# Raw weight loads over three buffer rings, a final norm whose last square is summed by TensorE, and three preparations held behind the bank sums

## The chip, the cores and the metric

The kernel runs on one core of one Trainium2 chip. The metric is the device time of one execution in microseconds (us): median of three runs. Besides the timed runs there is one profiled execution, from which all rows of the trace come.

## What is computed

One decoder layer on `x` of 1 x 1024 positions x 1024 channels, in float32:

```
h = rmsnorm(x, norm1_w);  proj = h @ w_in
A: short convolution, gated delta rule, gated norm     B: dilated window attention
x = x + concat(A, B) @ w_out
h = rmsnorm(x, norm2_w)
u = causal_dwconv(h @ w_up, ffn_conv_w)                # 2 x 2816 channels
gate, up = u[..., :2816], u[..., 2816:]
x = x + (silu(gate) * up) @ w_down                     # 2816 -> 1024: the down projection
out = rmsnorm(x, final_norm_w)
```

Only the last two lines, the down projection and the final norm, are touched by the change.

## The kernel before

Everything is held transposed: 128 channels on the partitions, positions along the free axis. Every matrix product is made three times over: an operand is split into a high part (a rounded copy made by ScalarE, ACT) and a low part (the rest, a subtraction on VectorE, DVE), and TensorE (PE) multiplies high x high, high x low and low x high (`mm3`). So each operand of the down projection has to be prepared: loaded by a DMA that SyncE (SP) issues, combined, copied by ACT, subtracted by DVE.

**The down projection** (`mlp_down`) is one level of a fast (seven product) matrix scheme. The 22 blocks of 128 channels are paired into HT = 11 steps `j`. There are four stages of 11 steps. In stages 0, 1 and 2 each step feeds two products, one into the four PSUM banks `pa`, one into the four banks `pb` (two tags of two banks each; all banks are called `dw` in the trace); a product of a step is 12 matmuls of 128x512. Stage 3 has one product, into `pa`; its last LAST = 5 steps are done bank by bank in two halves of 256 positions (`last_product`), so that the final norm of the left half can run while the right half is multiplied. At the end of a stage each of the eight banks is added into the residual stream in SBUF (`add_to`, rows `x1h<-x1h,dw`, one per bank), and the first matmul of the next stage into a bank has to wait until that bank has been read: these are the bank sums.

**Preparation.** `prep(stage, j)` is called one step ahead of its products. Stage 0 loads weights (`wd`, 512 KB) and activations (`r`, from the DRAM buffer `upark`), and splits both. Stage 1 loads a weight pair `wd` and half a pair `wa` (256 KB), makes two combinations of weights and one of activations (`t2 = q1 - r0`), splits three tiles, and updates `r`. Stage 2 loads two pairs and combines them. Stage 3 loads half a pair. The split tiles are called `pr` and take turns over 11 tags (`PTAGS`, nine in pool tag Xb, two in Xa); a `pr` buffer is free again when PE has read it for the last time.

**Raw weight buffers.** Three tags of the pool `wp` have two buffers of 4 KB per partition each: `wst`, `whi`, `wlo`. Stage 0 used `wst` and `whi` in turn, stage 1 `wst` for `wd`, `whi` for `wa` and `wlo` for `t2`, stage 2 `wst` and `whi`, stage 3 `wst` and `whi` in turn. In the up projection before it, `wst` and `whi` hold raw weights and `wlo` the tile `u2`. A load into a buffer starts when the last reader of its former content is done.

**The order of instructions.** PE's order is fixed by the program (an issue token on every matmul). The order on DVE, ACT and SP is made by the tile framework's scheduler, which walks a timeline of its own when the program is built and issues what it thinks is ready; each engine then runs its list strictly in order. `after(inst, anchor)` adds an ordering edge for that scheduler: `inst` comes later than `anchor` in the list, with no new semaphore on the same engine. SP's list holds all DMA issues: one that waits for a buffer holds up those behind it.

**The end.** For a half of 256 positions `complete` squares each of the eight row blocks on ACT and adds the squares into `rstdB` on DVE; `final_norm` sums over the partitions by matmuls with a column of ones (`ps<-ones,rstdB`), makes the scale on DVE and GpSimd (POOL, `rs`), spreads it over the partitions by transposes (`ps<-ident,rs`), and eight DVE instructions scale the row blocks (`x1h<-x1h,fw,ps`), each followed by a DMA to the output (`out_xT`, 128 KB each).

Of the kernel before, what the change touches and what calls it, by code (L numbers as in the profile page):

```python
# [7 lines left out]
F32 = mybir.dt.float32  # L8
# [136 lines left out]
def hybrid_layer(tc, I, out):  # L145
# [7 lines left out]
    po_ = Engine(wv, nc.gpsimd, "gpsimd", 0.15, 0.0021)  # L153
    sy = Engine(wv, nc.sync, "sync", 0.05, 0.00142, 2.2)
    es = ExitStack()
    cp = es.enter_context(tc.tile_pool(name="cp", bufs=1))
# [1195 lines left out]

    def raw_tile(name, tag, src, n=2):
        t = tile_(wp, [P, n, 512], F32, name, tag, 2)
        sy.dma_start(t, src)
        return t
# [10 lines left out]
    def split_pair(src):  # L1367
        hi, lo = [], []
        for d in (hi, lo):
            d.append(A("pr", PTAGS[pcount[0] % len(PTAGS)], F32R, (P, 2, 512)))  # L1370
            pcount[0] += 1
        split_block((hi[0], lo[0]), src)
        return [(hi[0][:, i, :], lo[0][:, i, :]) for i in range(2)]

    def split_one(src, tag=None):
        if tag is None:
            tag = PTAGS[pcount[0] % len(PTAGS)]
            pcount[0] += 1
        t = A("pr", tag, F32R, (P, 2, 512))
        b = t[:, 0, :], t[:, 1, :]  # L1380
        split_block(b, src)
        return b

    def prep(stage, j):
        if stage == 0:

            g = raw_tile("wd", ("wst", "whi")[j % 2], wd_rows(j, 0))
            r = R1[j] = acts("r1", R1TAGS[j], j, 0)
# [4 lines left out]
        elif stage == 1:  # L1393

            u = raw_tile("wd", "wst", wd_rows(j, 1))
            a = raw_tile("wa", "whi", wd_rows(j, 0)[:, 0:1], 1)
            r, q = R1[j], R2[j]
            sy.dma_start(q[:, 1, :], upark[HT + j][:, half(1)])
            t2 = tile_(wp, [P, 512], F32, "t2", "wlo", 2)
            ve.tensor_tensor(u[:, 1, :], u[:, 0, :], u[:, 1, :], op=OP.add)  # L1400
            ve.tensor_tensor(u[:, 0, :], u[:, 1, :], a[:, 0, :], op=OP.subtract)
            ve.tensor_tensor(t2, q[:, 1, :], r[:, 0, :], op=OP.subtract)
            w = split_pair(u)
            ops[stage, j] = [(w[0], split_one(t2)), (w[1], split_one(r[:, 0, :]))]
            ve.tensor_tensor(r[:, 1, :], r[:, 1, :], t2, op=OP.subtract)
        elif stage == 2:

            g = raw_tile("wd", "wst", wd_rows(j, 0))
            u = raw_tile("wd", "whi", wd_rows(j, 1))
            ve.tensor_tensor(g, g, u, op=OP.subtract)  # L1410
            ve.tensor_tensor(g[:, 1, :], g[:, 0, :], g[:, 1, :], op=OP.add)
            r = R2[j]
            ve.tensor_tensor(r[:, 0, :], r[:, 1, :], r[:, 0, :], op=OP.subtract)
            ops[stage, j] = list(zip(split_pair(g), split_pair(r)))
        else:

            a = raw_tile("wa", ("wst", "whi")[j % 2], wd_rows(j, 1)[:, 1:2], 1)
            ops[stage, j] = [(split_one(a[:, 0, :]), split_one(R1[j][:, 1, :], R2TAGS[j]))]
# [15 lines left out]
    def add_to(pd, m, hh, sl):  # L1434
        x = x1h[m][:, part(m, hh, sl)]
        ve.tensor_tensor(x, x, pd[:, sl], op=OP.add)

    def complete(m, hh, sl):

        sp_ = part(m, hh, sl)  # L1440
        x = x1h[m][:, sp_]
        sq = tile_(sp, [P, 512], F32, "sq3", "t2", 2)
        ac.activation(sq[:, sl] if m else rstdB[:, sp_], x, AF.Square)
        if m:
            ve.tensor_tensor(rstdB[:, sp_], rstdB[:, sp_], sq[:, sl], op=OP.add)

    def final_norm(hh, sl, tags, between=None):
        n_ = (sl.stop - sl.start) // P
        ss = bank(tags[0])
        for c in range(n_):  # L1450
            o = 512 * hh + sl.start + c * P
            mm(ss[:, c:c + 1], rstdB[:, o:o + P], ones[:, :1], 0.215)
        rs = tile_(sp, [P, 4], F32, "rs3", "rs3", 2)
        ve.tensor_scalar(rs[:, :n_], ss[:, :n_], 1.0 / 1024, EPS, op0=OP.mult, op1=OP.add)
        rsqrt(rs[:, :n_], rs[:, :n_], n_)
        if between is not None:
            between()
        pb = bank(tags[1])
        for c in range(n_):
            tp(pb[:, c * P:(c + 1) * P], rs[:, c:c + 1].to_broadcast([P, P]))  # L1460
        for m in range(8):
            x = x1h[m][:, part(m, hh, sl)]
            ve.scalar_tensor_tensor(x, x, fw[:, m:m + 1], pb[:, :sl.stop - sl.start], op0=OP.mult, op1=OP.mult)
            sy.dma_start(out[m * P:(m + 1) * P, part(m, hh, sl)], x)

# [5 lines left out]
    def mlp_down():  # L1471
# [30 lines left out]
        def last_product(i, sl):  # L1502
            for j in range(HT - LAST, HT):
                down(pa[i], i, ops[3, j][0], sl, False, j == HT - 1)
            add_to(pa[i], 4 + i, 0, sl)
            complete(4 + i, 0, sl)


# [3 lines left out]
        last_product(0, right)  # L1512
        final_norm(0, left, ("hf", "ch"), lambda: last_product(1, right))
        for i in (2, 3):
            last_product(i, right)
        final_norm(0, right, ("hf", "ch"))

# [71 lines left out]
```

## Time and profile before

| | us |
|---|---|
| median of three runs | 1220.66 (1220.21 to 1220.72) |
| the profiled execution | 1219.28 |
| its span, first to last instruction | 1217.5 |
| PE busy in the span | 1200.4 |
| DVE busy | 946.1 |
| ACT busy | 574.6 |
| POOL busy | 52.1 |
| first product of the down projection | at 988.74 |
| last product of the down projection ends | at 1205.35 |

All times in rows are us from the start of the span. A row of a timeline gives start, duration, engine, source line, operation, the tiles written and read (buffer numbers left out), the shape, how many instructions were merged into the row, and in brackets the idle time of the engine just before it and what ended it. Lines L139, L141, L189 and L193 are helpers through which every operation passes, so rows are told apart by their tiles. SPq is the queue of DMA issues. A DVE row of 128x512 lasts 0.68 to 0.69 us, but the next one starts 0.60 us after it; one of 128x1024 lasts 1.22 and the next starts after 1.14: what counts in a queue is the step from start to start.

### The profile page before, as it was taken

How to read it: one execution, taken by the hardware profiler on the slowest of the kernel's cores; microseconds unless marked ns; L12 is line 12 of the kernel's file. 1: busy time of each engine (PE TensorE's matmuls, PEld its weight loads, DVE VectorE, ACT ScalarE, POOL GpSimd, SP SyncE). 2: the span in 40 equal slices, each digit the busy share in tenths (PEclk: the TensorE clock that was granted, in tenths of full speed). 3: DMA queues.
4: the chain of work that ended last, by engine and by line, in shares of the span. 5: the costliest groups of instructions: out<-in, count | busy, mean ns of one | idle time of the engine just before them, and what ended most of it. 6: DMA issues, size and time to landing. Idle time of an engine off the chain costs nothing.

```text
span 1217.5 us, 18285 instructions
## 1 busy us (share of the span) xinstructions
PE 1200.4 (99%) x7064; PEld 986.3 (81%) x7064; DVE 946.1 (78%) x1459; ACT 574.6 (47%) x1124; POOL 52.1 (4%) x46
## 2 busy tenths in 40 slices
PE   9999999999999999999999999999999999999996
PEld 7878887889777778888888888888888888787886
DVE  7675965566477686767989988989889889899875
ACT  7393344356344453655544544445444444344441
POOL 0311010003100000000000000000000000000000
PEclk9999999999999999999999999999999999999998
DMA  7425252335634213444213223132231496555623
GB/s 231 107 79 165 83 145 85 116 127 164 214 102 129 88 36 107 173 139 144 82 57 105 68 88 104 52 104 68 89 104 53 141 376 234 165 177 177 181 87 139
DMA packets 85799, 154.81 MB, mean 127 GB/s; under 512 B 21168, under 2 KB 36304, under 8 KB 85712
## 3 DMA queue, kind: packets, MB, share of 16 engines
q1 hardware_dynamic: 85712, 153.64, 39.4%
q8 instruction: 55, 0.90, 0.3%
q14 instruction: 32, 0.26, 0.1%
HBM read 117.68 MB, written 35.93 MB: 126 GB/s over the span
## 4 chain that ended last, share of the span: by engine, by line
PE 87%; DVE 6%; DMA 3%; issue 2%; ACT 2%; SPq 0%; POOLq 0%; POOL 0%; DVEq 0%; ACTq 0%
PE ps L189 44%; PE pa L189 20%; PE pc L189 10%; PE dw L189 10%; PE ps L193 3%; DMA wd<-in_wd 2%; DVE pr L139 2%; DVE x1h L139 1%; DVE wd L139 1%; DVE kT L139 1%; ACT dec L139 1%; PE warm L189 1%; DVE wlo L139 0%; DMA r<-upark 0%; ACT sq L141 0%
## 5 line engine op out<-in xcount | busy, mean ns | idle before, releaser
L189 PE MATMUL dw<-pr 128*128 128x512 f32 (+1 forms) x984 | 213.0, 377 | 2.2 <-DVE x1h L139 2.2
L189 PEld LDWEIGHTS dw<-pr 128*128 128x128 f32 x984 | 176.1, 188 | 38.0 <-DVE x1h L139 4.4
L189 PE MATMUL ps<-xhi,whi 128*128 128x512 f32 x384 | 158.5, 413 | 0.0
L189 PE MATMUL ps<-xhi,wlo 128*128 128x512 f32 x384 | 150.3, 391 | 0.0
L189 PE MATMUL ps<-xlo,whi 128*128 128x512 f32 x384 | 150.1, 391 | 0.0
L189 PE MATMUL pa<-T,pair 128*128 128x512 f32 x528 | 127.1, 389 | 0.0
L189 PEld LDWEIGHTS pa<-T,pair 128*128 128x128 f32 x528 | 99.0, 188 | 20.5
L189 PEld LDWEIGHTS ps<-xhi,wlo 128*128 128x128 f32 x384 | 72.1, 188 | 15.7 <-DVE wlo L139 0.2
L189 PEld LDWEIGHTS ps<-xhi,whi 128*128 128x128 f32 x384 | 72.3, 188 | 14.9 <-issue 1.4
L189 PEld LDWEIGHTS ps<-xlo,whi 128*128 128x128 f32 x384 | 72.4, 189 | 12.1 <-DVE xlo L139 0.3
L139 ACT ACTIVATE u<-pa 128x512 f32<-128x512 f32 x44 | 26.3, 599 | 109.5 <-PE pa L189 109.5
L139 ACT ACTIVATE whi<-wst 128x1024 fp32r<-128x1024 f32 (+2 forms) x41 | 41.9, 1021 | 73.8 <-PE ps L189 65.9
L139 DVE SCALAR_TENSOR_TENSOR y<-xu,fcw,y 128x1023 f32<-128x1023 f32 (+1 forms) x44 | 56.3, 1281 | 22.1 <-ACT y L139 22.0
L141 ACT ACTIVATE sm<-sm,mx 128x128 f32<-128x128 f32 (+7 forms) x64 | 35.4, 555 | 60.0 <-DVE mx L141 60.0
L189 PE MATMUL pa<-T,S 128*128 128x512 f32 x264 | 63.4, 389 | 0.0
L189 PE MATMUL pa<-B,A 128*128 128x512 f32 x264 | 63.4, 389 | 0.0
L189 PE MATMUL pc<-T,S 128*128 128x512 f32 x264 | 63.4, 389 | 0.0
L189 PE MATMUL pc<-B,pair 128*128 128x512 f32 x264 | 63.4, 389 | 0.0
L139 DVE TENSOR_TENSOR wst<-wst 128x512 f32<-128x512 f32 x88 | 60.5, 687 | 0.9
L189 PE MATMUL ps<-B,pair 128*128 128x512 f32 x252 | 60.5, 389 | 0.0
L139 ACT ACTIVATE pr<-wd 128x1024 fp32r<-128x1024 f32 x33 | 34.9, 1058 | 50.5 <-DVE wd L139 28.0
L139 DVE TENSOR_TENSOR wlo<-wst,whi 128x1024 fp32r<-128x1024 f32 (+2 forms) x41 | 48.2, 1175 | 13.1 <-ACT whi L139 13.1
(245 smaller groups left out, 2360.9 us busy)
## 6 DMA issues: line engine op xcount, KB each, us to landing
wst<-in_wu SPq DMA_DIRECT2D x44, 512.0 KB, 3.7
wd<-in_wd SPq DMA_DIRECT2D x44, 512.0 KB, 4.3
upark<-y SPq DMA_DIRECT2D x22, 512.0 KB, 3.7
wst<-in_wi SPq DMA_DIRECT2D x21, 512.0 KB, 3.7
r<-upark SPq DMA_DIRECT2D x11, 512.0 KB, 7.9
r<-upark SPq DMA_DIRECT2D x22, 256.0 KB, 7.0
wa<-in_wd SPq DMA_DIRECT2D x22, 256.0 KB, 2.7
wst<-in_wv SPq DMA_DIRECT2D x8, 512.0 KB, 3.5
```

The costliest lines, as they stand in the source:

```text
L139: return getattr(eng, op)(*a, **kw)
L141: return getattr(eng, op)(*a, **kw)
L189: tc.stamp_issue_order_token(nc.tensor.matmul(dst, lhs, rhs, start=start, stop=stop, **kw).ins, TOKEN)
L193: tc.stamp_issue_order_token(nc.tensor.transpose(dst, src, ident if idt is None else idt).ins, TOKEN)
```

## The change

Four things change; the products and their order on PE stay as they are.

1. All raw weight tiles of the down projection take turns over the three tags (`wd_tile`), six buffers in all. In stage 1 the tile `wa` is a whole pair, of which one half takes the load and the other takes `t2`, so that a step of stage 1 holds two buffers where it held three.
2. Three preparations get an ordering edge to the last bank sum of the stage before (`behind`): the making of `t2` of step (1, 4) and the last low part of step (1, 1) come after sum number 7, the last of stage 0; the last low part of step (2, 1) comes after sum number 15, the last of stage 1.
3. The final norm is cut into `mean_of`, `turned` and `scale_out`. The scalings of the left half are placed by hand: row blocks 0 to 3, then the bank sum of product 2 of the right half, row blocks 4 to 6, the bank sum of product 3, row block 7. The square of the very last row block is not added into `rstdB`: TensorE sums it by two further matmuls with ones into the same bank.
4. The last eight output DMAs are issued from SP and ACT in turn (`queues=(sy, sa)`).

```diff
--- before.py
+++ after.py
@@ -152,6 +152,7 @@
     ua = Engine(wv, nc.scalar, "scalar", 0.12, 0.00085, first=tc.high_priority)
     po_ = Engine(wv, nc.gpsimd, "gpsimd", 0.15, 0.0021)
     sy = Engine(wv, nc.sync, "sync", 0.05, 0.00142, 2.2)
+    sa = Engine(wv, nc.scalar, "actq", 0.05, 0.00142, 2.2)
     es = ExitStack()
     cp = es.enter_context(tc.tile_pool(name="cp", bufs=1))
     wp = es.enter_context(tc.tile_pool(name="wp", bufs=1))
@@ -1350,8 +1351,14 @@
     pcount = [0]
     LAST = 5
 
-    def raw_tile(name, tag, src, n=2):
-        t = tile_(wp, [P, n, 512], F32, name, tag, 2)
+    wcount = [0]
+
+    def wd_tile(name="wd"):
+        wcount[0] += 1
+        return tile_(wp, [P, 2, 512], F32, name, ("wst", "whi", "wlo")[wcount[0] % 3], 2)
+
+    def raw_tile(src):
+        t = wd_tile()
         sy.dma_start(t, src)
         return t
 
@@ -1369,7 +1376,7 @@
         for d in (hi, lo):
             d.append(A("pr", PTAGS[pcount[0] % len(PTAGS)], F32R, (P, 2, 512)))
             pcount[0] += 1
-        split_block((hi[0], lo[0]), src)
+        lows.append(split_block((hi[0], lo[0]), src)[1])
         return [(hi[0][:, i, :], lo[0][:, i, :]) for i in range(2)]
 
     def split_one(src, tag=None):
@@ -1378,13 +1385,18 @@
             pcount[0] += 1
         t = A("pr", tag, F32R, (P, 2, 512))
         b = t[:, 0, :], t[:, 1, :]
-        split_block(b, src)
+        lows.append(split_block(b, src)[1])
         return b
+
+    lows, added = [], []
+
+    def behind(inst, n):
+        after(inst, added[n], "the banks of the stage are added first")
 
     def prep(stage, j):
         if stage == 0:
 
-            g = raw_tile("wd", ("wst", "whi")[j % 2], wd_rows(j, 0))
+            g = raw_tile(wd_rows(j, 0))
             r = R1[j] = acts("r1", R1TAGS[j], j, 0)
             ops[stage, j] = list(zip(split_pair(g), split_pair(r)))
             q = R2[j] = A("r2", R2TAGS[j], shape=(P, 2, 512))
@@ -1392,29 +1404,37 @@
             ve.tensor_tensor(r[:, 0, :], q[:, 0, :], r[:, 0, :], op=OP.subtract)
         elif stage == 1:
 
-            u = raw_tile("wd", "wst", wd_rows(j, 1))
-            a = raw_tile("wa", "whi", wd_rows(j, 0)[:, 0:1], 1)
+            u = raw_tile(wd_rows(j, 1))
+            both = wd_tile("wa")
+            sy.dma_start(both[:, 0, :], wd_rows(j, 0)[:, 0, :])
             r, q = R1[j], R2[j]
             sy.dma_start(q[:, 1, :], upark[HT + j][:, half(1)])
-            t2 = tile_(wp, [P, 512], F32, "t2", "wlo", 2)
+            t2 = both[:, 1, :]
             ve.tensor_tensor(u[:, 1, :], u[:, 0, :], u[:, 1, :], op=OP.add)
-            ve.tensor_tensor(u[:, 0, :], u[:, 1, :], a[:, 0, :], op=OP.subtract)
-            ve.tensor_tensor(t2, q[:, 1, :], r[:, 0, :], op=OP.subtract)
+            ve.tensor_tensor(u[:, 0, :], u[:, 1, :], both[:, 0, :], op=OP.subtract)
+            inst = ve.tensor_tensor(t2, q[:, 1, :], r[:, 0, :], op=OP.subtract)
             w = split_pair(u)
             ops[stage, j] = [(w[0], split_one(t2)), (w[1], split_one(r[:, 0, :]))]
+            if j == 4:
+                behind(inst, 7)
+            if j == 1:
+                behind(lows[-1], 7)
             ve.tensor_tensor(r[:, 1, :], r[:, 1, :], t2, op=OP.subtract)
         elif stage == 2:
 
-            g = raw_tile("wd", "wst", wd_rows(j, 0))
-            u = raw_tile("wd", "whi", wd_rows(j, 1))
+            g = raw_tile(wd_rows(j, 0))
+            u = raw_tile(wd_rows(j, 1))
             ve.tensor_tensor(g, g, u, op=OP.subtract)
             ve.tensor_tensor(g[:, 1, :], g[:, 0, :], g[:, 1, :], op=OP.add)
             r = R2[j]
             ve.tensor_tensor(r[:, 0, :], r[:, 1, :], r[:, 0, :], op=OP.subtract)
             ops[stage, j] = list(zip(split_pair(g), split_pair(r)))
+            if j == 1:
+                behind(lows[-1], 15)
         else:
 
-            a = raw_tile("wa", ("wst", "whi")[j % 2], wd_rows(j, 1)[:, 1:2], 1)
+            a = wd_tile("wa")
+            sy.dma_start(a[:, 0, :], wd_rows(j, 1)[:, 1, :])
             ops[stage, j] = [(split_one(a[:, 0, :]), split_one(R1[j][:, 1, :], R2TAGS[j]))]
 
     def load_x1(mg, hh):
@@ -1433,35 +1453,52 @@
 
     def add_to(pd, m, hh, sl):
         x = x1h[m][:, part(m, hh, sl)]
-        ve.tensor_tensor(x, x, pd[:, sl], op=OP.add)
-
-    def complete(m, hh, sl):
+        added.append(ve.tensor_tensor(x, x, pd[:, sl], op=OP.add))
+        return added[-1]
+
+    def complete(m, hh, sl, apart=False):
 
         sp_ = part(m, hh, sl)
         x = x1h[m][:, sp_]
         sq = tile_(sp, [P, 512], F32, "sq3", "t2", 2)
         ac.activation(sq[:, sl] if m else rstdB[:, sp_], x, AF.Square)
+        if apart:
+            return sq
         if m:
             ve.tensor_tensor(rstdB[:, sp_], rstdB[:, sp_], sq[:, sl], op=OP.add)
 
+    def mean_of(hh, sl, tag, more=None):
+        n_ = (sl.stop - sl.start) // P
+        ss = bank(tag)
+        for src, o in ((rstdB, 512 * hh + sl.start), (more, sl.start)):
+            if src is not None:
+                for c in range(n_):
+                    mm(ss[:, c:c + 1], src[:, o + c * P:o + c * P + P], ones[:, :1], 0.215,
+                       src is rstdB and (c == 0 or more is None), src is more or more is None, skip_group_check=True)
+        rs = tile_(sp, [P, 4], F32, "rs3", "rs3", 2)
+        uv.tensor_scalar(rs[:, :n_], ss[:, :n_], 1.0 / 1024, EPS, op0=OP.mult, op1=OP.add)
+        rsqrt(rs[:, :n_], rs[:, :n_], n_)
+        return rs
+
+    def turned(rs, sl, tag):
+        pb = bank(tag)
+        for c in range((sl.stop - sl.start) // P):
+            tp(pb[:, c * P:(c + 1) * P], rs[:, c:c + 1].to_broadcast([P, P]))
+        return pb
+
+    def scale_out(hh, sl, pb, ms=range(8), queues=(sy,), anchor=None):
+        for m in ms:
+            x = x1h[m][:, part(m, hh, sl)]
+            inst = ve.scalar_tensor_tensor(x, x, fw[:, m:m + 1], pb[:, :sl.stop - sl.start], op0=OP.mult, op1=OP.mult)
+            if anchor is not None:
+                after(inst, anchor, "the sums of the last banks go first")
+            queues[m % len(queues)].dma_start(out[m * P:(m + 1) * P, part(m, hh, sl)], x)
+
     def final_norm(hh, sl, tags, between=None):
-        n_ = (sl.stop - sl.start) // P
-        ss = bank(tags[0])
-        for c in range(n_):
-            o = 512 * hh + sl.start + c * P
-            mm(ss[:, c:c + 1], rstdB[:, o:o + P], ones[:, :1], 0.215)
-        rs = tile_(sp, [P, 4], F32, "rs3", "rs3", 2)
-        ve.tensor_scalar(rs[:, :n_], ss[:, :n_], 1.0 / 1024, EPS, op0=OP.mult, op1=OP.add)
-        rsqrt(rs[:, :n_], rs[:, :n_], n_)
+        rs = mean_of(hh, sl, tags[0])
         if between is not None:
             between()
-        pb = bank(tags[1])
-        for c in range(n_):
-            tp(pb[:, c * P:(c + 1) * P], rs[:, c:c + 1].to_broadcast([P, P]))
-        for m in range(8):
-            x = x1h[m][:, part(m, hh, sl)]
-            ve.scalar_tensor_tensor(x, x, fw[:, m:m + 1], pb[:, :sl.stop - sl.start], op0=OP.mult, op1=OP.mult)
-            sy.dma_start(out[m * P:(m + 1) * P, part(m, hh, sl)], x)
+        scale_out(hh, sl, turned(rs, sl, tags[1]))
 
     STEPS = [(s_, j) for s_ in range(4) for j in range(HT)]
     XLOADS = {6: (0, 0), 12: (1, 0), 14: (0, 1), 16: (1, 1)}
@@ -1502,18 +1539,22 @@
         def last_product(i, sl):
             for j in range(HT - LAST, HT):
                 down(pa[i], i, ops[3, j][0], sl, False, j == HT - 1)
-            add_to(pa[i], 4 + i, 0, sl)
-            complete(4 + i, 0, sl)
-
+            total = add_to(pa[i], 4 + i, 0, sl)
+            return total, complete(4 + i, 0, sl, sl.start > 0 and i == 3)
 
         left, right = slice(0, 256), slice(256, 512)
         for i in range(4):
             last_product(i, left)
         last_product(0, right)
-        final_norm(0, left, ("hf", "ch"), lambda: last_product(1, right))
-        for i in (2, 3):
-            last_product(i, right)
-        final_norm(0, right, ("hf", "ch"))
+        rs = mean_of(0, left, "hf")
+        last_product(1, right)
+        pl = turned(rs, left, "ch")
+        scale_out(0, left, pl, range(0, 4))
+        third, _ = last_product(2, right)
+        scale_out(0, left, pl, range(4, 7), anchor=third)
+        fourth, more = last_product(3, right)
+        scale_out(0, left, pl, range(7, 8), anchor=fourth)
+        scale_out(0, right, turned(mean_of(0, right, "hf", more), right, "ch"), queues=(sy, sa))
 
     wv.add(0, norms())
     wv.add(1, gates())
```

## The prediction

> **What bounds the kernel now.** I first read who PE waited for in the stretch from the down projection to the end, then PE's own timeline there. The columns of the first view are total, times and longest wait; the view is cut to this stretch.
>
> ```profile
> span 1217.5 us, 18285 instructions
> PE dw L189 <- DVE x1h L139: 2.2, 5, 0.6
> 988.74 61.41 PE L189 MATMUL dw<-pr 128*128 128x512 f32 x270
> 1050.76 0.96 PE L189 MATMUL dw<-pr 128*128 128x512 f32 x3 [0.61 <-DVE x1h L139]
> 1051.96 3.06 PE L189 MATMUL dw<-pr 128*128 128x512 f32 x12 [0.23 <-DVE x1h L139]
> 1055.55 57.42 PE L189 MATMUL dw<-pr 128*128 128x512 f32 x252 [0.53 <-DVE x1h L139]
> 1113.36 3.06 PE L189 MATMUL dw<-pr 128*128 128x512 f32 x12 [0.39 <-DVE x1h L139]
> 1116.89 68.99 PE L189 MATMUL dw<-pr 128*128 128x512 f32 x303 [0.47 <-DVE x1h L139]
> ```
>
> PE is the bound, and it never waits for an operand: it stops five times, 0.61 + 0.23 + 0.53 = 1.37 us around the end of stage 0 and 0.39 + 0.47 = 0.86 around the end of stage 1, each time for a bank sum, 2.23 in all. After its last product (1201.52 + 3.83 = 1205.35, a row of the tail below) a chain of 12.15 us follows. The change can win there: at two stage ends and in that tail. A product matmul takes 61.41 / 270 = 0.227, so a step of 24 takes 5.45, a product of 12 takes 2.72, and stage 0 (264) ends at 988.74 + 60.0 = 1048.7.
>
> Why the sums are late shows DVE's timeline at the first stage end, and ACT's and SP's ahead of it:
>
> ```profile
> 1037.68 1.06 ACT L139 ACTIVATE pr<-wd 128x1024 fp32r<-128x1024 f32 x1 [4.15 <-PE dw L189]
> 1041.71 0.38 SPq L139 DMA_DIRECT2D wd<-in_wd  x1
> 1045.88 0.69 DVE L139 TENSOR_TENSOR wd<-wd 128x512 f32<-128x512 f32 x1 [2.14 <-DMA wd<-in_wd]
> ...
> 1047.69 1.28 DVE L139 TENSOR_TENSOR x1h<-x1h,dw 128x512 f32<-128x512 f32 x2
> 1048.88 1.22 DVE L139 TENSOR_TENSOR pr<-wd,pr 128x1024 fp32r<-128x1024 f32 x1
> 1050.02 0.68 DVE L139 TENSOR_TENSOR x1h<-x1h,dw 128x512 f32<-128x512 f32 x1
> ...
> 1053.61 0.68 DVE L139 TENSOR_TENSOR t<-r,r 128x512 f32<-128x512 f32 x1
> 1054.21 0.69 DVE L139 TENSOR_TENSOR pr<-r,pr 128x512 fp32r<-128x512 f32 x1
> 1054.82 0.68 DVE L139 TENSOR_TENSOR x1h<-x1h,dw 128x512 f32<-128x512 f32 x1
> DVE wd L139 <- DMA wd<-in_wd: 13.8, 12, 2.7
> ```
>
> The first bank was full at about 1048.7 - 5.45 + 0.68 = 1043.9, but DVE stood still for 2.14 us until a raw weight load landed, and started that sum at 1047.69 (a row that merges sums 1 and 2). The third sum (1050.02) ends at 1050.70, while PE wants its bank 6 matmuls into stage 1, at 1050.1: the stall of 0.61. Two preparations (`t<-r,r`, `pr<-r,pr`) stand ahead of the eighth: the stall of 0.53. Over the down projection up to 1190 DVE waited 13.8 us in 12 pieces for raw weights (last row, DVE's waits).
>
> **Change 1 and 2 at the first stage end.** The change turns two buffers per kind into six shared ones and puts the `t2` of step (1, 4) and the last low part of (1, 1) behind the eighth sum. I walk through DVE's new list there; steps from start to start are 1.28 - 0.68 = 0.60 for 128x512, and 1050.02 - 1048.88 = 1.14 for 128x1024. The low part of (1, 0) needs ACT's copy, which waits for a buffer that PE gives back, as now at 1037.68; so it is done at 1037.68 + 1.06 + 1.22 = 1040.0. It frees the buffer of the load for (1, 3), which lands 1045.88 - 1041.71 = 4.2 us later, at 1044.2. The new list stands still for that too, but then has only a combination and a low part ahead of the first sum: 1045.4. Then follow a combination, sum 2 (1046.6), a low part of 1.14, sum 3 (1048.3), a low part, sum 4 (1049.5), sums 5 to 8 (1050.1 to 1051.9). Done 0.68 later, sum 3 is there 1.1 us before PE wants it, sum 4 (wanted at 1050.8) 0.6, sum 8 (wanted at 1053.5) 0.9. So all three stalls go, with about half a microsecond to spare. Behind the sums the held low part of (1, 1) runs at 1052.5; PE wants it with the second product of that step, at 1048.7 + 5.45 + 2.72 = 1056.9. What waits behind it on DVE belongs to steps (1, 2) and later. The edges cost nothing while that slack of 4 us lasts.
>
> **The second stage end.**
>
> ```profile
> 1109.09 1.88 DVE L139 TENSOR_TENSOR x1h<-x1h,dw 128x512 f32<-128x512 f32 x3
> ...
> 1115.02 1.22 DVE L139 TENSOR_TENSOR pr<-r,pr 128x1024 fp32r<-128x1024 f32 x1
> 1116.15 0.68 DVE L139 TENSOR_TENSOR x1h<-x1h,dw 128x512 f32<-128x512 f32 x1
> ```
>
> Without stalls stage 1 now ends 1.4 us earlier, at 1108.7, so DVE must be earlier by as much. In the list of before stand 55 short and 14 long instructions between the last sum of stage 0 and the first of stage 1: 55 x 0.60 + 14 x 1.14 = 49.0; it took 1055.4 to 1109.1, so 4.7 us of waits. The new list has 54 and 15, 49.5 us, from 1052.5: the first sum comes at 1102.0 plus waits. Sum 3 follows 4.1 us behind sum 1 (a low part, two combinations and two sums stand between), lasts 0.68 and is wanted at 1108.7 + 1.36 = 1110.1: up to 3.3 us of waits do no harm. Loads now have three steps of lead instead of two, 5.45 us more for a transfer of 4.2; the waits that are left are for `pr` buffers, which PE hands back at its own pace. I take 2 us. The low part of (2, 1) that stood ahead of the eighth sum (1115.02) goes behind it, at about 1110, and is wanted at 1114.2. So 0.86 goes too. Together **-2.2**, with bounds of 0 (the stalls stay as large) and -2.23.
>
> **Stage 0.** Here the ring order moves loads on SP's queue: the weights of step 6 are issued before the activations of steps 1, 3 and 5, and those of step 4 wait for `u2` of the last up tile, holding up what stands behind them on SP.
>
> ```profile
> 985.00:1021.00 36.00, 36.00 (x161) 29.78 (x160) 33.49 (x38) 17.87 (x18) 0.00 (x0) 1.00 0.99 358
> 1003.85 1.22 DVE L139 TENSOR_TENSOR pr<-r,pr 128x1024 fp32r<-128x1024 f32 x1
> ```
>
> The DMA engines are 0.99 busy at 358 GB/s (last columns), so 512 KB put ahead cost 1.5 us. The low part of (0, 3) ends at 1005.07, just when PE wants it (988.74 + 3 x 5.45 = 1005.1). But in the new list four short instructions (the `t2` and `r` updates of steps 0 and 1) no longer stand before it, 2.4 us, and ACT copies `xu` before it waits for step 1's activations. A load late by 1.5 us is covered: 0, bounds 0 to +1.5.
>
> **Change 3 and 4, the tail.**
>
> ```profile
> 1201.92 3.22 DVE L139 SCALAR_TENSOR_TENSOR x1h<-x1h,fw,ps 128x256 f32<-128x256 f32 x8
> 1205.05 0.42 DVE L139 TENSOR_TENSOR rstdB<-rstdB,sq 128x256 f32<-128x256 f32 x1
> 1205.39 0.74 DVE L139 TENSOR_TENSOR x1h<-x1h,dw 128x256 f32<-128x256 f32 x2
> 1206.34 0.96 DVE L139 TENSOR_TENSOR rstdB<-rstdB,sq 128x256 f32<-128x256 f32 x2 [0.21 <-ACT sq L139]
> 1199.04 0.61 PE L189 MATMUL ps<-ones,rstdB 128*128 128x1 f32 x4
> 1199.51 2.03 PE L189 MATMUL dw<-pr 128*128 128x256 f32 x15
> 1201.38 0.38 PE L193 MATMUL ps<-ident,rs 128*128 128x128 f32 x2
> 1201.52 3.83 PE L189 MATMUL dw<-pr 128*128 128x256 f32 x30
> 1207.44 0.98 PE L189 MATMUL ps<-ones,rstdB 128*128 128x1 f32 x4 [2.10 <-DVE rstdB L139]
> 1209.53 0.69 PE L193 MATMUL ps<-ident,rs 128*128 128x128 f32 x2 [1.10 <-POOL rs L139]
> 1205.89 0.75 ACT L139 ACTIVATE sq<-x1h 128x256 f32<-128x256 f32 x2 [3.38 <-DVE x1h L139]
> 1207.40:1209.50 2.10, 0.98 (x4) 0.93 (x4) 0.16 (x1) 0.00 (x0) 0.69 (x1) 0.50 0.00 0
> L139 SPq DMA_DIRECT2D out_xT<-x1h x8: 332/390/404, 1210.8 to 1214.1; - x8
> ```
>
> The hand-placed scalings move the last bank sum hardly at all: four scalings of (1205.05 - 1201.92) / 8 = 0.39, an add into `rstdB`, the sum of product 2, three scalings, an add, each add 1205.39 - 1205.05 = 0.34, and then the last sum at 1201.92 + 7 x 0.39 + 3 x 0.34 = 1205.67, where it now starts at 1206.13 - 0.42 = 1205.71. Its square is ready at about 1206.6 (now 1206.64). Now two adds follow it, up to 1207.30, and the ones matmuls start 0.14 later. In the new version they follow the square directly, 1206.73 at the earliest: **-0.7**. The four extra ones matmuls (on `rstdB`) run before that.
>
> The ones matmuls took 0.98 at a granted clock of 0.50 (window row), and 0.61 at full clock (1199.04). Starting 0.7 earlier, behind ones matmuls at about 1205.9, I let them run at full clock: **-0.4**. The transposes (0.69, and 0.38 at full clock) I leave as they are. The Trainium skill, "TensorE: Matmul & The Clock Gate", section "What's actually happening", says that the clock falls only after a free-running window of about 3.4 us without activity. The trace has half clock from 2.1 us after the last product on, so the figure does not fit here. By the rule the transposes would stay fast as well, and the time would be 0.3 lower.
>
> The eight last issues go out every (1214.1 - 1210.8) / 7 = 0.47 us, while DVE scales every 0.39; the last is issued 1214.1, 0.6 later than its scaling allows (1210.8 + 7 x 0.39 = 1213.5). With two queues each has 0.78 per issue: **-0.6**. What an issue costs on ACT no row shows; at the median of SP (0.39) it fits, and if ACT's issues had to wait for SP's the gain would be 0. If each took three times SP's, 1.2 us, the last would start 0.9 + 3 x 1.2 = 4.5 after the first scaling can be sent, against 3.3 now: +1.2. I take SP's median, the nearest row. The Trainium skill, "DMA: Bandwidth & Descriptors", section "Issuing engines are not separate DMA queues", says that queues of several engines share the same 16 DMA engines and save issue time alone. 128 KB every 0.39 us is 336 GB/s, under the 358 of above, so issue time is what is short here.
>
> **The sum.** -2.2 - 0.7 - 0.4 - 0.6 = -3.9. The profiled execution took 1219.28 (span 1217.5 and 1.8 around it), 1.4 below the median of the runs; it would become 1215.4, and the median 1220.66 becomes **1216.8**.
>
> **Rivals.**
> - *The sums stay late* (0.14). DVE's list still has a load wait right ahead of the sums of stage 0, with 0.6 us to spare, and the waits of stage 1 may stay at 4.7. For it: the waits for `pr` buffers are not shortened. Against it: both walks have slack, and the 13.8 us of load waits are what rings shorten. The stage ends then give 0 to -0.9: 1218.1 to 1219.0, about 1218.7.
> - *Stage 0 runs dry* (0.08). If the two moved loads delay activations beyond what DVE gained, PE stops at steps 3 and 4 for 2 x 1.5 = 3.0 us each, DVE comes late to the first stage end as well, and only the tail is won: +6.0 - 1.7 = +4.3, 1225.0. It decides from a delay of 2.4 us at step 3. For it: the DMA share of 0.99 and the low part ready with nothing to spare. Against it: the new order puts that low part earlier in the list.
> - *The change does not do what it says* (0.03): the sums stay as late as they are, and issues on ACT of 1.2 us cost 1.2 in place of the 0.6, against 1.1 from the norm: 1220.66 + 1.2 - 1.1 = 1220.8.
>
> **How the numbers follow.** The forecast has 0.75. A measurement here tells about 0.2%, 2.4 us, from no change: the forecast is faster than that (1216.8 against 1218.2); the late sums are within it but for a fifth of them, as is the last rival; the dry stage is slower. That gives 0.78 faster, 0.14 same, 0.08 slower. The range starts at 1215.6: with fast transposes 1216.5, and 0.9 less since one execution lay 1.4 from the median. It reaches to 1219.2, over the late sums; outside are the dry stage and the last rival.
>
> **What the profile would show.** Right: no PE row with an idle time from `x1h` at the ends of stages 0 and 1, the first sum of stage 0 near 1045.4 and of stage 1 near 1104, the `sq` ones matmuls near 1204.5 (2.2 earlier than 1206.7), the last output issue 3.3 us less an issue behind the first. Wrong: PE rows with idle time from `pr` in stage 0, sums of stage 1 that end after PE wants them, or ACT issues that last a microsecond.

## The result, and the profile after

| | before | changed |
|---|---|---|
| median of the runs | 1220.55 us | 1215.48 us |
| lowest to highest | 1217.41 to 1220.72 | 1213.86 to 1216.67 |
| the profiled execution, own time (span) | 1219.28 (1217.5) | 1215.80 (1214.0) |

The ratio is 0.9958 with an interval of 0.9947 to 0.9968, so the change saves 5.1 us (3.9 to 6.5). The forecast had the direction and the places right, and its 3.9 is at the small end of that interval; 1215.48 lies 0.12 below the range.

Who PE waited for from the down projection to the end, in the changed kernel (total, times, longest):

```profile
PE dw L190 <- DVE x1h L139: 0.8, 1, 0.8
PE ps L190 <- DVE rstdB L139: 0.6, 1, 0.6
PE ps L190 <- ACT sq L139: 0.2, 1, 0.2
```

The wait for bank sums (`x1h`) went from 2.2 us in 5 pieces to 0.8 in one, and the 2.1 for `rstdB` in the tail became 0.6 and 0.2. DVE's waits for raw weights, which the rings were to shorten, went from 13.8 us in 12 pieces to this (985 to 1190 us):

```profile
DVE wd L139 <- DMA wd<-in_wd: 4.5, 3, 2.2
```

At the same time its waits for `pr` buffers that PE gives back rose from 0.4 to 6.7 us. PE's timeline, of the changed kernel, has this (start, length, count; the bracket is idle time ahead of the row):

```profile
981.19 2.88 PE L190 MATMUL ps<-B,pair 128*128 128x512 f32 x12
984.31 3.02 PE L190 MATMUL pa<-T,pair 128*128 128x512 f32 x12 [0.24 <-ACT u L139]
...
989.89 121.61 PE L190 MATMUL dw<-pr 128*128 128x512 f32 x534
1112.32 72.37 PE L190 MATMUL dw<-pr 128*128 128x512 f32 x318 [0.82 <-DVE x1h L139]
...
1200.33 3.83 PE L190 MATMUL dw<-pr 128*128 128x256 f32 x30
1204.71 0.58 PE L190 MATMUL ps<-ones,rstdB 128*128 128x1 f32 x4 [0.55 <-DVE rstdB L139]
1205.45 0.61 PE L190 MATMUL ps<-ones,sq 128*128 128x1 f32 x4 [0.17 <-ACT sq L139]
1207.16 0.43 PE L194 MATMUL ps<-ident,rs 128*128 128x128 f32 x2 [1.10 <-POOL rs L139]
```

Four things are to be seen. The three stops at the end of stage 0 are gone: one row runs through them (it swallows a stop of 0.12 at 1052.05). One stop of 0.82 is left at the end of stage 1. Ahead of the down projection there is a stop that the kernel before did not have, 0.24 us for ACT's copy `u`. And in the tail the ones matmuls on the last square start 1.29 us after the last product (1205.45 against 1200.33 + 3.83), where they started 2.09 after it; ones matmuls and transposes are both shorter.

DVE's timeline of the changed kernel at the two stage ends says why the first is cured in this execution and the second is not:

```profile
1045.97 0.69 DVE L139 TENSOR_TENSOR wd<-wd 128x512 f32<-128x512 f32 x1 [2.18 <-DMA wd<-in_wd]
1047.18 0.68 DVE L139 TENSOR_TENSOR x1h<-x1h,dw 128x512 f32<-128x512 f32 x1
...
1051.31 3.07 DVE L139 TENSOR_TENSOR x1h<-x1h,dw 128x512 f32<-128x512 f32 x5
1054.30 0.68 DVE L139 TENSOR_TENSOR pr<-r,pr 128x512 fp32r<-128x512 f32 x1
...
1102.90 1.23 DVE L139 TENSOR_TENSOR wd<-wd 128x1024 f32<-128x1024 f32 x1 [1.70 <-DMA wd<-in_wd]
...
1107.52 0.68 DVE L139 TENSOR_TENSOR x1h<-x1h,dw 128x512 f32<-128x512 f32 x1
...
1109.85 1.82 DVE L139 TENSOR_TENSOR wd<-wd 128x512 f32<-128x512 f32 x2
1111.59 3.67 DVE L139 TENSOR_TENSOR x1h<-x1h,dw 128x512 f32<-128x512 f32 x6
```

At 1054.30 stands the held low part, behind the eight sums. At the end of stage 1 the row at 1109.85 is two combinations of weights for steps (2, 3) and (2, 4), 1.74 us, and the third sum (1111.59) stands behind them.

### The profile page after: what moved, and what is told of

Same layout as the page of the kernel before. It is cut to its first block, busy times and chain, and to the rows that moved or that the text cites. A ratio compares the mean times of both kernels' runs of the same rounds, so it can differ in the third digit from the quotient of the medians.

```text
span 1214.0 us, 18278 instructions
## 1 busy us (share of the span) xinstructions
PE 1199.1 (99%) x7068; PEld 985.9 (81%) x7068; DVE 945.8 (78%) x1458; ACT 574.3 (47%) x1124; POOL 50.1 (4%) x46
## 4 chain that ended last, share of the span: by engine, by line
PE 91%; DVE 4%; ACT 2%; issue 2%; DMA 1%; SPq 0%; POOLq 0%; POOL 0%; DVEq 0%; ACTq 0%
PE ps L190 44%; PE pa L190 20%; PE dw L190 15%; PE pc L190 10%; PE ps L194 3%; DVE kT L139 1%; DVE x1h L139 1%; ACT dec L139 1%; DMA wd<-in_wd 1%; DMA xt<-in_xT 1%; DVE wlo L139 0%; ACT sq L141 0%; DVE xr L139 0%; DVE pr L139 0%; DVE wd L139 0%
## 5 line engine op out<-in xcount | busy, mean ns | idle before, releaser
L139 ACT ACTIVATE pr<-r 128x1024 fp32r<-128x1024 f32 (+1 forms) x44 | 36.3, 838 | 47.3 <-PE dw L190 29.2
```

Source lines behind the costliest of these rows:

```text
L139: return getattr(eng, op)(*a, **kw)
```

## The experiments

**Each part alone.** E1 takes the kernel before and gives it the new last norm:

```
 E1: prep(), raw_tile() and split_*() as before; mean_of, turned, scale_out, last_product as changed
```

> The kernel before with the last norm of the changed one (parts 3 and 4 alone: last square summed by ones, shared queues); rings and edges left out. Theory A (the tail is worth what its own rows show, 12.15 to 9.85 us from last product to span end): 2.3 us less than the kernel before, and the five stops of PE at the two stage ends stay, 2.2 us in brackets. Theory B (the tail is worth the 1.7 of the prediction, and the part beyond it lies ahead of the down projection): 1.7 less. In both the transposes of the last norm should take near 0.43 us and not 0.69.

Measured: 1219.14 us (11 runs) against 1221.06 for the kernel before, ratio 0.9986 (0.9977 to 0.9995), 1.7 us. From last product to span end it took 9.61 us, 2.5 less than the 12.15; its five stops are there (2.86 in brackets, where 2.2 was expected). Transposes took 0.43. Both theories are within the interval; the trace is with A.

E2 takes the changed kernel and gives it the old last norm:

```
 E2: final_norm, last_product and complete as before; rings and edges as changed
```

> The changed kernel with the last norm of the kernel before: rings and edges alone. Theory A (a stop costs its bracket and some 0.2 us of restart): first to last product takes 2.3 us less than the 216.6 before, though one stop of about 0.8 stays at the end of stage 1, and the new ACT wait at the turn from up to down costs 0.5: net 1.8 less. Theory B (a stop costs its bracket alone): 1.4 less between first and last product, net 0.9 less. The tail should take 12.15 us again, with ones matmuls of 0.98.

Measured: 1217.09 us, ratio 0.9972 (0.9961 to 0.9984), 3.4 us. The products took 213.47 us, 3.1 less than 216.60, with one stop; the wait for `u` was there (0.51). So the rings and edges are worth more than their brackets, theory A and beyond it. One expectation failed, in the tail, PE's timeline of E2:

```profile
1199.07 3.83 PE L190 MATMUL dw<-pr 128*128 128x256 f32 x30
1205.00 0.58 PE L190 MATMUL ps<-ones,rstdB 128*128 128x1 f32 x4 [2.10 <-DVE rstdB L139]
```

The old norm, starting as late as before (idle 2.10), ran its ones matmuls in 0.58 and not 0.98, and its tail took 11.40. The clock there is not set by how late they start; the last section returns to it.

**How typical the profiles were.** E5 and E6 are the kernel before, E7 the changed kernel, all without an edit.

> The kernel before, unchanged, profiled a second time. Open is whether the one profile on which the prediction was built was a typical execution: its own time 1219.28 is below nearly all of the runs, which reach from 1219.5 to 1222.3. Theory A (the stops at the stage ends change from execution to execution, and the profiled one had few): products from first to last take more than 216.6 us, 217 to 218, as in the run of the tail alone, with brackets over 2.23. Rival B (executions differ ahead of the down projection): 216.6 again, and the first product starts later than 988.7 by what the time is longer. The half clock of the tail begins after a multiple of 3.413 us of full clock, as in all traces so far.

> The same once more, for the spread: under theory A the brackets at the two stage ends differ by some tenths from the second profile; under rival B they agree and the first product's start differs.

> The changed kernel, unchanged, profiled a second time. Theory A: the stop at the end of stage 1 stays, since it follows from the order of DVE's list, between 0.4 and 0.9 us; the wait for u at the turn comes and goes between 0 and 0.5. Products take 213.4 to 214.3. Rival B: products 214.3 again and only the start differs.

Measured: 1221.10, 1219.11 and 1215.76 us. PE's timeline of E5:

```profile
989.87 61.59 PE L189 MATMUL dw<-pr 128*128 128x512 f32 x270
...
1115.21 3.03 PE L189 MATMUL dw<-pr 128*128 128x512 f32 x12 [1.13 <-DVE x1h L139]
```

Of the 1.8 us that E5 is longer than the first profile, 1.13 lies ahead of the first product (989.87 against 988.74, rival B) and 0.70 in the products (217.30 against 216.60, theory A: the stop at 1115.2 is 1.13 where it was 0.39). So both are true. E6 has its first product at 988.58 and products of 216.59, as the first profile, with 1.62 us in brackets at the stage ends (E5 2.76, theory A). One more of its stops is not at a stage end:

```profile
1005.67 46.03 PE L189 MATMUL dw<-pr 128*128 128x512 f32 x200 [0.24 <-DVE pr L139]
```

It is 73 matmuls in, where step 3 begins: the low part that the prediction saw ready with nothing to spare came late here. That PE never waits for an operand is true of the first profile, not of every execution of the kernel before. E7, the changed kernel, by PE and DVE:

```profile
988.64 61.38 PE L190 MATMUL dw<-pr 128*128 128x512 f32 x270
1050.78 0.97 PE L190 MATMUL dw<-pr 128*128 128x512 f32 x3 [0.76 <-DVE x1h L139]
1051.97 59.46 PE L190 MATMUL dw<-pr 128*128 128x512 f32 x261 [0.23 <-DVE x1h L139]
1112.29 10.04 PE L190 MATMUL dw<-pr 128*128 128x512 f32 x43 [0.85 <-DVE x1h L139]
```

```profile
1045.90 0.69 DVE L139 TENSOR_TENSOR wd<-wd 128x512 f32<-128x512 f32 x1 [2.17 <-DMA wd<-in_wd]
1047.11 0.68 DVE L139 TENSOR_TENSOR x1h<-x1h,dw 128x512 f32<-128x512 f32 x1
```

Here PE began its products 1.25 us earlier than in the first profile of the changed kernel, while DVE came out of its load wait at nearly the same moment (1045.90 and 1045.97): two of the three stops of stage 0 are back. Part of what the first profile showed was thus its late first product. My expectation of at most 214.3 was wrong; it took 215.48. The cure of stage 0 has no margin in such an execution.

**Edges and rings apart.** E8 leaves the edges out, E9 leaves the rings out:

```
 E8: def behind(inst, n): pass
 E9: E1 with the three calls of behind(); raw_tile(name, tag, src) with two buffers a kind, as before
```

> The changed kernel without its three edges: rings and new tail alone. Theory A (the sums were late since DVE came late out of its load waits, and the rings alone cure that): the stops at both stage ends are as in the changed kernel, the time within 0.5 us of 1215.5. Rival (the order of DVE's list right at the sums decides): PE stops around 1052 to 1056 again, up to 1 us in brackets and 0.3 a stop, and the time is 1 to 2 us longer than the changed kernel's.

> The kernel before with the three edges and the new last norm, but its two buffers per kind of raw weight kept: beside the run of the tail alone it tells what the edges do without the rings. Theory A (edges and rings work only together: with two buffers DVE still comes out of a load wait when the banks are full): most of the stops stay, products take 216 to 217 us, and the time is within 1 us of the 1219.1 of the tail alone. Rival (the edges are the whole of it): products take 214 to 215 and the time is near 1216.

Measured: E8 1216.94 us, ratio 0.9970 (0.9958 to 0.9982); E9 1218.12, ratio 0.9983 (0.9973 to 0.9992). PE's timelines, E8 first:

```profile
1054.20 56.07 PE L190 MATMUL dw<-pr 128*128 128x512 f32 x246 [0.39 <-DVE x1h L139]
1112.24 4.66 PE L190 MATMUL dw<-pr 128*128 128x512 f32 x18 [1.97 <-DVE x1h L139]
1117.56 4.60 PE L190 MATMUL dw<-pr 128*128 128x512 f32 x19 [0.66 <-DVE x1h L139]
```

```profile
1051.16 0.96 PE L190 MATMUL dw<-pr 128*128 128x512 f32 x3 [0.61 <-DVE x1h L139]
1052.36 58.37 PE L190 MATMUL dw<-pr 128*128 128x512 f32 x255 [0.24 <-DVE x1h L139]
1111.52 2.31 PE L190 MATMUL dw<-pr 128*128 128x512 f32 x9 [0.79 <-DVE x1h L139]
1114.96 7.32 PE L190 MATMUL dw<-pr 128*128 128x512 f32 x31 [1.13 <-DVE x1h L139]
```

Without the edges the changed kernel stops at 1054.2, 1112.2 and 1117.6, so E8's theory A fell. Its rival, the order of DVE's list right at the sums, holds for the first of these stops. The largest, 1.97, has both causes ahead of it: a load wait of 2.76 us that ended at 1103.41, and two combinations and a low part between the first two sums. The median is 1.5 us above the changed kernel's, but the intervals overlap. Without the rings the edges remove only the third stop of stage 0, and the products take 217.18 us (E9's theory A, a little above its 216 to 217).

What each part is worth alone is not settled. By the ratios, set against the 0.9986 of the tail alone, the rings take off another 2.0 us, the edges 0.4 and both together 3.4, and intervals of such differences are over a microsecond wide to each side. By the traces the products take 216.95 with the rings alone and 217.18 with the edges alone, no less than with neither (216.97, the mean of four), and 213.94 with both (the mean of five). E8's six runs lie between 1215.49 and 1218.15, and its one trace is of a slow one among them (1217.49). The traces thus speak for E9's theory A, that the two work only together; how much the rings give alone stays open.

**The terms of the tail.** E10 puts the last square back on DVE's add, E11 gives the last eight stores to SP alone:

```
 E10: complete(4 + i, 0, sl)                      # was: complete(4 + i, 0, sl, sl.start > 0 and i == 3)
 E11: scale_out(0, right, turned(...))            # was: ..., queues=(sy, sa))
```

> The changed kernel, but the last square is added on DVE ahead of the ones matmuls, as in the kernel before. Theory A: ones matmuls start 2.1 us after the last product instead of 1.29 on the square, and the tail from last product to span end grows from 9.85 to 10.5 or 10.7; where a tick of the clock (multiples of 3.413 us from where full clock began) falls between 1.9 and 4 us after the last product, the transposes are at half clock and it is 0.3 more. Rival (the square was not what held the norm): the tail stays at 9.9.

> The changed kernel, but the last eight stores are all issued by SP. Theory A: issues every 0.48 us again against scalings every 0.39, the last issue 0.62 later, and 0.24 more behind it: the tail grows from 9.85 to 10.5 to 10.7. Rival (the 16 DMA engines, shared by both issuers, set the end): the tail stays within 0.2 of 9.85.

Measured: 1215.37 and 1215.42 us, both within their intervals of the changed kernel (ratios 0.9957, 0.9944 to 0.9970, and 0.9959, 0.9945 to 0.9973): half a microsecond is below what the runs tell. The traces tell it. PE's timeline of E10, and the last stores of the changed kernel and of E11 (ns least/median/most, first and last start):

```profile
1205.07 0.58 PE L190 MATMUL ps<-ones,rstdB 128*128 128x1 f32 x4 [1.85 <-DVE rstdB L139]
```

```profile
L139 SPq DMA_DIRECT2D out_xT<-x1h x5: 332/332/333, 1205.3 to 1210.5; - x5
L139 ACTq DMA_DIRECT2D out_xT<-x1h x4: 338/338/380, 1208.5 to 1210.9; - x4
```

```profile
L139 SPq DMA_DIRECT2D out_xT<-x1h x8: 332/393/404, 1206.2 to 1209.5; - x8
```

E10's tail took 10.28 us, 0.44 more than 9.84; E11's took 10.30, 0.46 more. Both rivals fell; theory A has the direction in both, and its 10.5 to 10.7 is too large. The changed tail took between 9.6 and 10.0 in the eight traces that have it, so the sizes are better read at the steps themselves: E10's ones matmuls start 1.85 after the last product, the changed kernel's last ones 1.29, which is 0.56; E11's last store is issued 7.3 after it (1209.5 - 1202.21), the changed kernel's 6.7 (1210.9 - 1204.16), which is the 0.6 of the forecast. ACT issues a store in 0.34 us, as fast as SP.

**A better version.** E3 adds two edges to the changed kernel, E4 also starts the rings at another tag (`wst` in place of `whi`):

```
 E3, stage 2 of prep():
+            if j == 3: behind(two, 15)     # two: g[:, 1] = g[:, 0] + g[:, 1]
+            if j == 4: behind(one, 15)     # one: g = g - u
 E4, on top:
-    wcount = [0]
+    wcount = [2]
```

> The changed kernel with two more edges: the second combination of step (2, 3) and the first of step (2, 4) follow the last bank sum of stage 1, so that the third sum has nothing but the second ahead of it. Theory A (the third sum was late because of these two combinations, 1.7 us of DVE): the sum starts at about 1109.9 and PE's stop of 0.82 at the end of stage 1 goes, 1.0 us less than the changed kernel by bracket and restart. Rival (the raw weight load that DVE waited 1.7 us for, before the sums, sets it): the stop stays at 0.4 or more, and the time within 0.5.

> As the run before it, and the rings begin one place further, so that step (0, 1)'s weights go into a ring whose buffer is free early, as in the kernel before, and step (0, 2)'s into the one that the up projection gives back last. Theory A (the 0.24 us wait of PE for ACT's copy of u at the turn comes from that order): the wait goes, 0.5 us less than the run before it, about 1.5 less than the changed kernel. Rival (step (0, 2)'s weights now come late in turn): PE stops at the start of stage 0, idle from pr, and it is no faster.

> The version with two more edges and the ring begun one place further, unchanged, on the chip of these runs and with a second profile. Theory A: again no stop of PE between first and last product, 212.7 to 212.9 us, no wait for u at the turn, and 1213 to 1214 us, 2 less than the changed kernel. Rival (its first profile was a lucky execution): stops of 0.2 to 0.8 appear at a stage end, and the time is within 1 us of the changed kernel's.

Measured: E3 1214.32 us, ratio 0.9950 (0.9938 to 0.9963); E4 1213.22, ratio 0.9944 (0.9931 to 0.9956); E12, the same kernel as E4, 1213.55, ratio 0.9940 (0.9927 to 0.9953). E3's and E12's theories A hold in the traces. Two rows of DVE's timeline ahead of the end of stage 1, of E3 and then of E11, which lacks the two edges:

```profile
1102.50 1.23 DVE L139 TENSOR_TENSOR wd<-wd 128x1024 f32<-128x1024 f32 x1 [1.67 <-DMA wd<-in_wd]
1108.85 4.27 DVE L139 TENSOR_TENSOR x1h<-x1h,dw 128x512 f32<-128x512 f32 x7
```

```profile
1100.92 1.23 DVE L139 TENSOR_TENSOR wd<-wd 128x1024 f32<-128x1024 f32 x1 [0.72 <-DMA wd<-in_wd]
1109.61 3.67 DVE L139 TENSOR_TENSOR x1h<-x1h,dw 128x512 f32<-128x512 f32 x6
```

In E3 the load wait is as long as in the changed kernel, and the third sum starts at 1108.85 + 0.60 = 1109.45. Behind the two combinations, 1.74 later, it would have ended at 1111.9, where PE wanted it at about 1110.9 (534 matmuls after 989.36, and 0.46 for one stop of 0.19 on the way); so there the order took the stop away. In E11 the order is the old one, the load wait only 0.72, and PE does not stop either: there a shorter load wait was enough.

E4's theory A is not shown by its time. The wait for `u` was absent in E3 already, and the intervals of E3 and E4 overlap. What the trace shows is that the ring order moves the copy in question: ACT copies the weights of step (0, 1) at 982.71 in the changed kernel, just ahead of `u` at 983.68, and at 979.01 in E4, 2.72 ahead of `u`. E12's timeline of PE is one row:

```profile
988.76 193.28 PE L190 MATMUL dw<-pr 128*128 128x512 f32 x852
```

852 matmuls without a stop, and 212.74 us from first to last product, as in E4 (212.75). This is the fastest version here, by the ratios 6.8 (E4) and 7.3 us (E12) under the kernel before and about 2 under the changed one: its ten runs reach up to 1214.16, and of six of the changed kernel one lies below that.

## Why the prediction was right and where it failed

**The step that failed is the price of a stop.** I took each of PE's stops at its bracket, and made their sum, 2.23, the most that the stage ends could give. E12's row gives the pace, (193.28 - 0.39) / 851 = 0.2267 a matmul. By it E7's stop of 0.85 cost more: the matmul after it was due at 1051.97 + 261 x 0.2267 = 1111.14 and began at 1112.29, 1.15 late. Part of these 0.30 is how the row is drawn: a matmul is shown 0.39 long at a pace of 0.23, so a bracket starts counting 0.16 too late. Another 0.11 is that the first matmul after a stop, here the one at 1051.97, is 0.50 long instead of 0.39. The prediction's own rows had a sign of it: twelve matmuls behind a stop last 3.06 there, where twelve of this shape without one last 2.88 (981.19 above). Over 14 traces, products from first to last:

| trace | products, us | brackets, us | stops | us beyond 212.75 and brackets, a stop |
|---|---|---|---|---|
| before / E5 / E6 | 216.60 / 217.30 / 216.59 | 2.23 / 2.76 / 1.86 | 5 / 5 / 6 | 0.32 / 0.36 / 0.33 |
| E1 (preparations of before) | 217.39 | 2.86 | 5 | 0.36 |
| changed / E7 | 214.27 / 215.48 | 0.94 / 1.84 | 2 / 3 | 0.29 / 0.30 |
| E2 / E10 / E11 (preparations as changed) | 213.47 / 213.57 / 212.90 | 0.43 / 0.51 / 0 | 1 / 1 / 0 | 0.29 / 0.31 / - |
| E8 / E9 / E3 | 216.95 / 217.18 / 213.31 | 3.02 / 2.77 / 0.19 | 3 / 4 / 1 | 0.39 / 0.41 / 0.37 |
| E4 / E12 | 212.75 / 212.74 | 0 / 0 | 0 / 0 | - |

On the average of a trace a stop goes with its bracket and 0.3 to 0.4 us more. What is above 0.27 of it are mostly starts that come late with no bracket at all: E8's row at 1112.24 lasts 4.66, where 17 x 0.2267 + 0.50 is 4.35, and E11, without a stop, is 0.15 over 212.75. The five of the prediction's own profile stood for 3.85, not 2.23. With 3.85 in the sum the forecast would have been -5.5 and 1215.1, and the range would have reached 1.6 lower and held the result; that it would have come so near is luck in part, since not all stops went and the tail gave more.

**Stage ends: -2.2 forecast, -3.0 measured.** The four traces with the old preparations (E6's with its stop in stage 0) average 216.97, the five with the new ones 213.94. In brackets alone it is 2.43 to 0.74, 1.7, less than forecast, because stops stayed: two errors of opposite sign, of which the mis-priced stop is the larger.

**First stage end: the order was right, the load only in part.** From the end of the load wait to the first sum I foresaw 1.2 us, and it took 1047.18 - 1045.97 = 1.21; the third sum came 2.9 behind the first, as foreseen. What failed in two of five traces is the load. I let the low part that frees its buffer end at 1040.0 and the load land at 1044.2. E7 began its products when the prediction had it, at 988.64, and shows this:

```profile
1040.45 1.22 DVE L139 TENSOR_TENSOR pr<-wd,pr 128x1024 fp32r<-128x1024 f32 x1
1041.70 0.38 SPq L139 DMA_DIRECT2D wd<-in_wd  x1
```

That is as late as in the kernel before (1041.71), and so was the end of the wait, 1045.90. Counted from the first product the wait ended after 57.0 to 57.3 us in the three traces of the kernel before; foreseen was 1044.2 - 988.74 = 55.5. With the new preparations it was 55.0 to 55.5 in E2, E10 and E11, 56.1 in the changed kernel's first profile, where the 0.6 of slack was just used up and a stop of 0.12 was left, and 57.3 in E7, with two stops. Why the low part runs late in some executions stays open.

**Second stage end: wrong.** From the held low part to the first sum I allowed 49.5 us of work and 2 of waits, with 3.3 as the point from which it hurts. It took 1107.52 - 1054.30 = 53.2, so 3.7 of waits, 1.70 of them the load at 1102.90, which I had thought gone. That is 0.4 beyond the point; and the held low part itself came 0.65 later after the first product than foreseen (64.41 against 63.76). Together they are about the 1.1 that the stop of 0.82 costs. E3 took it away by moving work, not by shortening waits.

**Stage 0 and the turn.** No activation came late, as forecast:

```profile
985.00:1021.00 36.00, 36.00 (x161) 29.79 (x160) 33.42 (x37) 18.02 (x19) 0.00 (x0) 1.00 0.98 364
```

PE is busy for all of this window (its second figure), at nearly the DMA share of before (0.98 against 0.99). What I missed is one step earlier: the ring order puts step (0, 1)'s weights into a buffer that the last up tile frees late, ACT's copy of them stands ahead of `u<-pa`, and PE waits for `u`: the matmul at 984.31 was due at 981.19 + 12 x 0.2267 = 983.91. The wait was there in the changed kernel and E2 and not in E7, E3, E10 and E11; E4 and E12, which start the rings elsewhere, are also without it. E8, with the same ring order, has no such wait either. The first product came 0.54 late by it in the changed kernel (8.70 us behind the row at 981.19, where E7 has 8.16) and 0.81 in E2, on the mean of the five traces 0.3.

**The tail: -1.7 forecast, -2.3 measured against the first profile.** The earlier start of the ones matmuls was 0.80 (forecast 0.7; 0.56 with E10 as the control), their length 0.98 to 0.61, 0.37 (0.4). The issues gave 0.6 as forecast by the two profiles, and 0.46 with E11 as the control. Missing were 0.26 from the transposes, which I left at 0.69 and which took 0.43, and 0.24 behind the last issue, for which no run shows a cause (it is 2.9 to 3.1 us with the same code). I had set aside the Trainium skill's rule, "TensorE: Matmul & The Clock Gate", section "What's actually happening", a free-running window of about 3.4 us, because the trace had half clock from 2.1 us after the last product. That was in part a misreading of "free-running": the traces agree with a grid of that step, which starts anywhere against the last product. They do not agree with a window without activity, since windows with 1.4 to 1.5 us of products in them ended full clock (last section).

**The sum.** Means of the traces: -3.0 + 0.3 - 2.2 (11.96 on the mean of four traces with the old norm, 9.78 of eight with the new) = -4.9; the runs say -5.1. Taking the profile's own 1219.28 for 1220.66 was harmless, but its products were at the mild end. Of the rivals, the late sums came true in part (one stop stayed, more in E7), but not at their price; stage 0 did not run dry; ACT's issues did not cost a microsecond.

## What to carry to other kernels

A bracketed idle time is a lower bound of what a stop of PE costs: take the pace from a long row without stops and ask when the next matmul was due. A preparation that runs early, ahead of a sum that frees a bank, is free to move behind it; in these traces that paid only where more buffers also let the engine arrive in time, and the buffers did not pay without it either. One profile is one execution: here the first product alone moved by 1.3 us between two profiles of one kernel, enough to hide two stops or to show them. Where a ring order changes, look at the first element in it that meets another phase's buffers, and at which copy then stands at the head of a queue.

## What the runs showed of the hardware

The granted clock of PE falls at ticks of a fixed grid, counted from where it rose. Its record has one stretch of full clock per trace, and its length was 1201.49, 1204.90 or 1198.08 us in all 14 traces, 3.41 apart: 352, 353 or 351 times 3.413. Full clock began between 4.3 and 6.3 us of the span, so the grid lies elsewhere in each execution, and the drop came anywhere from 1.9 to 5.2 us after the last product, a width of one step. Rows of windows, of before, the changed kernel and E4, with the clock as third figure from the end:

```profile
1207.00:1207.50 0.50, 0.06 (x1) 0.09 (x1) 0.30 (x1) 0.00 (x0) 0.00 (x0) 0.83 0.19 64
```

```profile
1209.00:1209.50 0.50, 0.00 (x0) 0.00 (x0) 0.50 (x2) 0.00 (x0) 0.00 (x0) 0.88 0.85 281
```

```profile
1204.00:1204.50 0.50, 0.34 (x4) 0.25 (x3) 0.05 (x1) 0.00 (x0) 0.00 (x0) 0.89 0.13 43
```

The drops lie inside these windows, at 1207.33, 1209.38 and 1204.39, that is 1.99, 5.22 and 1.95 after the last product. In E4 the new norm's transposes therefore took 0.69 and in the changed kernel 0.43, with the same code. The window need not be idle for the clock to fall. In E4 the one that ended with the drop, 1200.98 to 1204.39, held products up to 1202.44, 1.46 us. In the changed kernel the one that ended a step before the drop, 1202.56 to 1205.97, held 1.60 us of them, with the same ones matmuls behind, and full clock went on. A gain of 0.2 to 0.4 us from full clock in such a tail belongs to the execution, not to the kernel; an earlier tail only makes it likelier.
